# First pieces of x on ScalarE's queue, a one-column warm tile, and 512-column last sums in a two-layer decoder trunk

## The chip, the cores and the metric

One Trainium2 chip; the kernel runs on one of its cores. The metric is the device time of one execution in microseconds, given as the median of several runs. TensorE (PE) does the matmuls and loads its weights in a stream of its own (PEld), VectorE is DVE, ScalarE is ACT, GpSimd is POOL, and SyncE (SP) issues DMAs. "L137" is line 137 of the kernel before.

## What is computed

The reference runs two layers over x of 256 tokens by 1024 columns. Each layer is a token mixer and a SwiGLU block, each followed by a residual and a layer norm:

```python
for l in range(DEPTH):          # DEPTH = 2
    mix = hybrid_mixer(x, w_in[l], w_branch_sb[l], w_branch_moba[l], w_out[l])
    x = layer_norm(DEEPNORM_ALPHA * x + mix, ln_mix_g[l], ln_mix_b[l])
    ffn = swiglu(x, w_ffn_gate[l], w_ffn_up[l], w_ffn_down[l])
    x = layer_norm(DEEPNORM_ALPHA * x + ffn, ln_ffn_g[l], ln_ffn_b[l])

def swiglu(x, w_gate, w_up, w_down):
    return (jax.nn.silu(x @ w_gate) * (x @ w_up)) @ w_down   # inner width 2816
```

The mixer projects x to the queries, keys and values of two kinds of attention and to two gates. Everything is float32.

## The kernel before

**Three matmuls for one product.** A float32 operand is cut into a high part, in a rounded float32 format (float32r), and the low rest. ACT casts the high part (`act`, L50-53), DVE subtracts it (`dve`, L55-58). A product is then three matmuls, high by high, high by low and low by high (`mm3`, L334). The page puts all of ACT's and DVE's work under L51 and L56, and nearly all matmuls under L328, so tiles are told apart by name.

**The weights** come in 244 granules of 128 x 1024 (512 KB). `WeightStream.load` (L132) issues each granule's DMA on SP's queue, the first four granules of all in two halves of 256 KB (`_pieces`, L127). Up to six raw granules are held (NRAW). `line` (L144) casts and subtracts each granule into a ring of ten. A planner (`Weave`) keeps an estimated time of each engine and thereby writes the order of the instructions by hand; on the chip each engine and each queue runs its own list in that order.

**The start.** x comes transposed in pieces, one tile `xT_raw` for each half of the tokens (t = 0, 1). `kcs` (L298) cuts a half in 256, 256 and 512 columns: pieces 0 and 1 are 128 KB, piece 2 is 256 KB. All six are issued on SP's queue, piece (0, 0) before everything, the others between the halves of the granules as `X_AFTER` says (L188, used in `between`, L302). Call the halves of granule 0 w0a and w0b, and so on. SP's order is: x(0,0), w0a, w0b, x(1,0), x(0,1), w1a, w1b, x(1,1), x(0,2), w2a, w2b, x(1,2), w3a, w3b, and on from there with whole granules.

Meanwhile TensorE multiplies zeros: `idle` is a 128 x 512 tile that DVE clears after two small memsets (L279-284), and `N_WARM` = 6 matmuls of it go to a scratch bank (L286-287). ACT runs a sigmoid on one column as its first work (L281).

The first projection (`l0pv`) uses granules 0 to 3. The first two (NWHOLE) are not cut in parts: `whole` (L358) multiplies raw by raw in float32, one such product being two matmul records in the trace. Its eight products, 16 records, run in the order x(0,0) by w0a, by w0b; x(1,0) by w0a, by w0b; then x(0,1) and x(1,1) by w1a and w1b. From granule 2 on `mm3` is used.

**The end.** The last product, by `w_down`, runs over 22 chunks of the inner width (NFC). Of the first 14 (22 less HOLD = 8) each is done for both token halves in turn (L837-840); the last 8 are done for half 0 first, then for half 1, so that the norm of half 0 (`last_norm`, L619) runs on DVE meanwhile. Half 0 sums into two banks of 512 columns (tile `l1pd`). In the last layer half 1 sums into three tiles (`l1pe`): 512 columns, 256 and 256 (L834-835). In `last_norm` for half 1 the remaining 8 chunks go to the 512 columns first, then to one 256, then to the other, and behind each part DVE adds the residual and takes the statistics (`bn_stats`) of those columns. Then follow the aggregate, two small operations on POOL, six operations on DVE and the three stores of that half.

Of the kernel before, what the change touches and what calls it, by code (L numbers as in the profile page):

```python
# [7 lines left out]
F32 = mybir.dt.float32  # L8
F32R = mybir.dt.float32r
AF = mybir.ActivationFunctionType  # L10
# [4 lines left out]
P = 128  # L15
# [8 lines left out]
NFC = D_FF // P  # L24
# [13 lines left out]
class Weave:  # L38
# [16 lines left out]
    def dve(self, e, n, f, *args, **kw):  # L55
        f(*args, **kw)  # L56
        self.dve_t = max(self.dve_t, e) + n / 960.0 + DVE_FIXED
        return self.dve_t + HOP

    def pool(self, e, f, *args, **kw):  # L60
        f(*args, **kw)
        self.pool_t = max(self.pool_t, e) + 0.3
        return self.pool_t + HOP
# [121 lines left out]
RING = 10 * GCOLS + LINES  # L185
NRAW = 6
NWHOLE = 2
X_AFTER = {(0, 1): ((1, 0), (0, 1)), (1, 1): ((1, 1), (0, 2)), (2, 1): ((1, 2),)}  # L188
NSPLIT = 10
HOLD = 8  # L190
N_WARM = 6
LEAD = 2
BACKLOG = 0.37
HOP = 0.21
# [19 lines left out]
def hybrid_trunk_kernel(ctx: ExitStack, tc: tile.TileContext, w, xT_in, x_in, ln_in,  # L214
                        ident_in, mask_in, rope_in, out):
    nc = tc.nc

    big = ctx.enter_context(tc.tile_pool(name="big", bufs=1))
# [10 lines left out]
    def unit(name, shape, dt=F32):  # L229
        return acts.tile(shape, dt, tag="u4", name=name)  # L230
# [10 lines left out]
    def bankM(name, shape):  # L241
        return psM.tile(shape, F32, tag="M", name=name)

    def bankC(name, shape):
        return psC.tile(shape, F32, tag="C", name=name)
# [13 lines left out]
    zero, mhalf = few[:, 0:1], few[:, 1:2]  # L259
# [8 lines left out]
    act, dve, pool = weave.act, weave.dve, weave.pool  # L268


    xT_raw = [unit(f"xT_raw{t}", [P, KC, P]) for t in range(2)]
# [2 lines left out]
    mask = const.tile([P, 2, P], F32, name="mask")  # L274
    warm = small.tile([P, 1], F32, tag="nmu", name="warm")

    nc.gpsimd.memset(ends, 0.0)
    nc.gpsimd.memset(ends[:, P - 1::2 * P], 1.0)
    nc.vector.memset(zero, 0.0)  # L279
    nc.vector.memset(mhalf, -0.5)  # L280
    nc.scalar.activation(warm, zero, AF.Sigmoid)  # L281

    idle = unit("idle", [P, 512], F32R)
    nc.vector.memset(idle.bitcast(F32), 0.0)
    busy = bankC("busy", [P, 512])
    for i in range(N_WARM):  # L286
        nc.tensor.matmul(busy, idle[:, :P], idle, start=True, stop=True)

    def load_xT(t, ks):
        nc.sync.dma_start(xT_raw[t][:, ks, :], xT_in[:, t, ks, :])  # L290

    def split_xT(t, ks):
        n = (ks.stop - ks.start) * P
# [3 lines left out]

    kcs = [slice(0, 2), slice(2, 4), slice(4, 8)]  # L298
    ws.side = weave.add(ws.line(), last=True)
    load_xT(0, kcs[0])  # L300

    def between(g, i):  # L302
        for t, k in X_AFTER.get((g, i), ()):
            load_xT(t, kcs[k])

    ws.load(4, between)
    for k in range(2):
        for t in range(2):
# [25 lines left out]
    def mm3(o, s_hi, s_lo, m_hi, m_lo, start, stop):  # L334
        mm(o, s_hi, m_hi, start, False)
        mm(o, s_hi, m_lo, False, False)
        mm(o, s_lo, m_hi, False, stop)
        weave.tick()
# [8 lines left out]
    def pe_done():  # L347
        return weave.t + HOP
# [50 lines left out]
    def token_out(o, g, t, s_hi, s_lo, first, last):  # L399

        hi, lo = ws.take(g)
        ts = slice(t * P, (t + 1) * P)
        for c0, ps in o:
            cs = slice(c0, c0 + ps.shape[-1])
            mm3(ps, s_hi[:, ts], s_lo[:, ts], hi[:, cs], lo[:, cs], first, last)
# [168 lines left out]
    halves = [slice(h * 512, (h + 1) * 512) for h in range(2)]  # L574

    def residual(e, x, cs, ps, sum_out=None):
        return dve(e, cs.stop - cs.start, nc.vector.scalar_tensor_tensor, x[:, cs], x[:, cs], ALPHA, ps,
                   op0=OP.mult, op1=OP.add, accum_out=sum_out)

    def scale_shift(e, x, cols, sub, op, scale, g, b, e_scale):  # L580

        for c in cols:
            dve(e, c.stop - c.start, nc.vector.scalar_tensor_tensor, x[:, c], x[:, c], sub, g[:, c],
                op0=op, op1=OP.mult)
        for c in cols:
            e = dve(e_scale, c.stop - c.start, nc.vector.scalar_tensor_tensor, x[:, c], x[:, c], scale,
                    b[:, c], op0=OP.mult, op1=OP.add)
            yield c, e

    def norm_line(name, t, junk, gb):  # L590

        x = xs[t]
        st = small.tile([P, 2], F32, tag="st", name=f"{name}_st{t}")
        nmu = small.tile([P, 1], F32, tag="nmu", name=f"{name}_nmu{t}")
        ve = small.tile([P, 1], F32, tag="ve", name=f"{name}_ve{t}")
        e = pe_done()
        for h in range(2):
            e = residual(e, x, halves[h], junk[:, h, :], st[:, h:h + 1])
        e = dve(e, 16, nc.vector.tensor_scalar, nmu, st[:, 0:1], st[:, 1:2], -1.0 / D, op0=OP.add, op1=OP.mult)
        e2 = act(e, D + 100, nc.scalar.activation, junk, x.rearrange("p (h c) -> p h c", h=2), AF.Square,  # L600
                 bias=nmu, accum_out=ve)
        e2 = pool(e2, nc.gpsimd.tensor_scalar, ve, ve, 1.0 / D, EPS, op0=OP.mult, op1=OP.add)
        e2 = pool(e2, nc.gpsimd.tensor_tensor, ve, ve, mhalf, op=OP.pow)
        ends = [e for _, e in scale_shift(e, x, halves, nmu, OP.add, ve, *gb, e2)]
        for h in range(2):
            yield ends[h] + MARGIN
            tp = bankC(f"{name}_tp{t}{h}", [P, 4, P])
            pe_after(ends[h])
            for j in range(4):
                transpose(tp[:, j, :], x[:, (4 * h + j) * P:(4 * h + j + 1) * P])  # L610
            ks = slice(h * 4, (h + 1) * 4)
            ts = slice(t * P, (t + 1) * P)
            e = pe_done()
            yield e
            xT_ready[t] = yield from split_line(xT_hi[:, ks, ts], xT_lo[:, ks, ts], tp, 512, e)
# [3 lines left out]
    def last_norm(name, t, banks, gb, down):  # L619

        x = xs[t]
        st = small.tile([P, 3, 6], F32, tag="bn", name=f"{name}_bn{t}", bufs=1)
        mv = small.tile([P, 2], F32, tag="mv", name=f"{name}_mv{t}", bufs=1)
        ve = small.tile([P, 1], F32, tag="ve", name=f"{name}_ve{t}")
        cols = [slice(c0, c0 + ps.shape[-1]) for c0, ps in banks]
        if t == 0:
            down(banks)
        for i, (c0, ps) in enumerate(banks):
            if t == 1:
                down([(c0, ps)])  # L630
            residual(pe_done(), x, cols[i], ps)
            e = dve(0.0, cols[i].stop - c0, nc.vector.bn_stats, st[:, i, :], x[:, cols[i]])
        e = dve(e, 16, nc.vector.bn_aggr, mv, st[:, :len(banks), :])
        e2 = pool(e, nc.gpsimd.tensor_scalar, ve, mv[:, 1:2], EPS, None, op0=OP.add)
        e2 = pool(e2, nc.gpsimd.tensor_tensor, ve, ve, mhalf, op=OP.pow)
        for c, _ in scale_shift(e, x, cols, mv[:, 0:1], OP.subtract, ve, *gb, e2):
            nc.sync.dma_start(out[t * P:(t + 1) * P, c], x[:, c])
# [17 lines left out]
    for l in range(DEPTH):  # L655
        G = l * NG_LAYER
        L = f"l{l}"
# [19 lines left out]
        else:  # L677
            for t in range(2):
                weave.finish(norms[:t + 1])
                pe_after(xT_ready[t])  # L680
                for j, put in enumerate((put_v, put_q)):
                    ps = bankM(f"{L}pvq{j}{t}", [P, WIDTH])
                    for i in range(4):
                        g = G + 4 * j + i
# [68 lines left out]
        for c in range(KC):  # L753
            g = G + 40 + c
# [3 lines left out]
            ps = bankM(f"{L}pb{c}", [P, 2, S])  # L758
# [7 lines left out]
            e = dve(0.0, S, nc.vector.tensor_add, mt[:, 0, :], mt[:, 0, :], mt[:, 1, :])  # L766
# [15 lines left out]
        def h_parts(c):  # L782
            return h_t[c // 4][0][:, c % 4, :], h_t[c // 4][1][:, c % 4, :]
# [27 lines left out]
        for t in range(2):  # L811
            weave.finish(norms[:t + 1])
            pe_after(xT_ready[t])
            for j in range(2):
                ps = bankM(f"{L}pft{t}{j}", [P, 512])
                for i in range(4):
                    g = G + 56 + 4 * j + i
# [4 lines left out]
        for c in range(NTOK_FC, NFC):  # L822
            ps = bankM(f"{L}pf{c}", [P, 2, S])
# [7 lines left out]
        acc = [banksB(f"{L}pd{t}") for t in range(2 if l < DEPTH - 1 else 1)]  # L831
        banks = [[(512 * h, a[:, h, :]) for h in range(2)] for a in acc]
        if l == DEPTH - 1:
            banks.append([(0, bankM(f"{L}pe0", [P, 512])), (512, bankM(f"{L}pe1", [P, 512])[:, :256]),  # L834
                          (768, bankC(f"{L}pe2", [P, 512])[:, :256])])
        g = G + 100
        for c in range(NFC - HOLD):  # L837
            for t in range(2):
# [1 line left out]
            ws.used(g + c)  # L840
        norms = []
        for t in range(2):
            def down(part, t=t):
                for c in range(NFC - HOLD, NFC):
                    token_out(part, g + c, t, *h_parts(c), False, c == NFC - 1)
                    if t == 1:
                        ws.used(g + c)
            if l < DEPTH - 1:
                down(banks[t])
                norms.append(weave.start(norm_line(f"{L}b", t, acc[t], gb)))  # L850
            else:
                last_norm(f"{L}b", t, banks[t], gb, down)
# [86 lines left out]
```

## Time and profile before

| what | value |
|---|---|
| median of 3 runs | 734.23 us (734.13 to 734.25) |
| profiled execution: its time / its span | 734.21 us / 732.4 us |
| mean granted TensorE clock in it | 0.998 |
| PE busy | 723.1 us (99%) |
| DVE busy / ACT busy | 515.6 us (70%) / 384.5 us (52%) |
| moved by DMA | 136.32 MB, mean 186 GB/s |

The span is what the trace covers; 1.81 us of the execution's time lie around it. PE stands at 9 tenths or more in all 40 slices of the page, so the time of this kernel is the sum of TensorE's work and of the few places where TensorE waits. The timeline lists, for each run of like instructions, the start, the time covered, engine, line, operation, and in brackets the idle time before it with what ended it. The chain of waits follows the work that ended last back in time. The times of single matmuls include a drain that overlaps the next one, so that costs of matmuls are read from the distance between starts.

### The profile page before, as it was taken

To read this page: it belongs to the slowest core of one execution; us is meant where nothing else is said; L and a number is where in the kernel's file an instruction comes from. 1 tells how busy PE (TensorE), PEld (TensorE's weight loads), DVE (VectorE), ACT (ScalarE), POOL (GpSimd) and SP (SyncE) were. 2 spreads that over 40 slices of the span, in tenths; PEclk is the share of its full clock that TensorE was granted. 3 is DMA by queue.
4 is the path that set the end of the run, shared out by engine and by line. 5 is a ranking of instruction groups with operands and counts; after the bars stand their busy time and mean duration, and the time that the engine had idled before them with its cause. 6 is when DMAs were issued, how large, how long until landed. Compare 5 with 4: busy or idle time off the path is not lost.

```text
span 732.4 us, 12739 instructions
## 1 busy us (share of the span) xinstructions
PE 723.1 (99%) x5136; PEld 664.7 (91%) x5136; DVE 515.6 (70%) x723; ACT 384.5 (52%) x570; POOL 14.8 (2%) x30
## 2 busy tenths in 40 slices
PE   9999999999999999999999999999999999999996
PEld 5898999998799999988889989999888999998885
DVE  4988877795886666644578897777578766656416
ACT  5755668743565455533356566675246645445300
POOL 0000000000000000000000000000010000000001
PEclk9999999999999999999999999999999999999999
DMA  8953553863586655476158425457436866554601
GB/s 319 353 202 116 163 191 122 263 241 117 176 279 211 198 201 186 160 273 215 57 177 286 144 96 190 147 158 257 161 115 223 264 203 193 186 172 129 244 1 57
DMA packets 39226, 136.32 MB, mean 186 GB/s; under 512 B 4480, under 2 KB 5504, under 8 KB 39168
## 3 DMA queue, kind: packets, MB, share of 16 engines
q1 hardware_dynamic: 39168, 135.51, 54.9%
q8 instruction: 40, 0.66, 0.3%
q14 instruction: 18, 0.15, 0.1%
HBM read 134.45 MB, written 1.05 MB: 185 GB/s over the span
## 4 chain that ended last, share of the span: by engine, by line
PE 95%; DVE 2%; issue 1%; ACT 1%; POOL 1%; POOLq 0%; DVEq 0%
PE l1pf L328 13%; PE l0pf L328 13%; PE l0pd L328 8%; PE l1pg L328 6%; PE l0pg L328 6%; PE l1pe L328 4%; PE l1pd L328 4%; PE l0pq L328 3%; PE l0pk L328 3%; PE l1pk L328 3%; PE l1pvq L328 3%; PE l1pb L328 3%; PE l0pb L328 3%; PE l1pw L328 2%; PE l0pw L328 2%; PE l0pft L328 2%
## 5 line engine op out<-in xcount | busy, mean ns | idle before, releaser
L56 DVE TENSOR_TENSOR wlo<-raw,whi 128x1024 fp32r<-128x1024 f32 (+1 forms) x244 | 292.1, 1214 | 77.1 <-ACT whi L51 74.2
L51 ACT CAST whi<-raw 128x1024 fp32r<-128x1024 f32 (+1 forms) x244 | 249.8, 1042 | 68.4 <-PE l0pd L328 19.1
L328 PE MATMUL l0pf<-xT_hi,whi 128*128 128x256 f32 x288 | 79.6, 276 | 0.0
L328 PE MATMUL l1pf<-xT_hi,whi 128*128 128x256 f32 x288 | 79.6, 276 | 0.0
L328 PE MATMUL l0pf<-xT_lo,whi 128*128 128x256 f32 x288 | 79.5, 276 | 0.0
L328 PE MATMUL l0pf<-xT_hi,wlo 128*128 128x256 f32 x288 | 79.5, 276 | 0.0
L328 PE MATMUL l1pf<-xT_lo,whi 128*128 128x256 f32 x288 | 79.5, 276 | 0.0
L328 PE MATMUL l1pf<-xT_hi,wlo 128*128 128x256 f32 x288 | 79.5, 276 | 0.0
L328 PEld LDWEIGHTS l0pf<-xT_lo,whi 128*128 128x128 f32 x288 | 54.1, 188 | 0.0
L328 PEld LDWEIGHTS l1pf<-xT_lo,whi 128*128 128x128 f32 x288 | 54.1, 188 | 0.0
L328 PEld LDWEIGHTS l1pf<-xT_hi,whi 128*128 128x128 f32 x288 | 54.1, 188 | 0.0
L328 PEld LDWEIGHTS l0pf<-xT_hi,whi 128*128 128x128 f32 x288 | 54.1, 188 | 0.0
L328 PEld LDWEIGHTS l0pf<-xT_hi,wlo 128*128 128x128 f32 x288 | 54.1, 188 | 0.0
L328 PEld LDWEIGHTS l1pf<-xT_hi,wlo 128*128 128x128 f32 x288 | 54.1, 188 | 0.0
L328 PE MATMUL l1pg<-xT_hi,whi 128*128 128x256 f32 x128 | 36.0, 281 | 0.0
L328 PE MATMUL l0pg<-xT_hi,whi 128*128 128x256 f32 x128 | 36.0, 281 | 0.0
L328 PE MATMUL l1pg<-xT_lo,whi 128*128 128x256 f32 x128 | 35.5, 277 | 0.0
L328 PE MATMUL l1pg<-xT_hi,wlo 128*128 128x256 f32 x128 | 35.5, 277 | 0.0
L328 PE MATMUL l0pg<-xT_lo,whi 128*128 128x256 f32 x128 | 35.5, 277 | 0.0
L328 PE MATMUL l0pg<-xT_hi,wlo 128*128 128x256 f32 x128 | 35.4, 277 | 0.0
L328 PE MATMUL l0pd<-whi,l0h_hi 128*128 128x512 f32 x88 | 34.4, 391 | 0.0
L328 PE MATMUL l0pd<-whi,l0h_lo 128*128 128x512 f32 x88 | 34.3, 389 | 0.0
(403 smaller groups left out, 1763.9 us busy)
## 6 DMA issues: line engine op xcount, KB each, us to landing
raw<-in_w_dram SPq DMA_DIRECT2D x240, 512.0 KB, 4.2
ln<-in_ln_dram SPq DMA_DIRECT2D x8, 512.0 KB, 6.2
raw<-in_w_dram SPq DMA_DIRECT2D x8, 256.0 KB, 4.9
x<-in_x_dram SPq DMA_DIRECT2D x2, 512.0 KB, 5.3
out_dram<-x SPq DMA_DIRECT2D x3, 256.0 KB, 2.0
xT_raw<-in_xT_dram SPq DMA_DIRECT2D x4, 128.0 KB, 4.4
xT_raw<-in_xT_dram SPq DMA_DIRECT2D x2, 256.0 KB, 4.8
out_dram<-x SPq DMA_DIRECT2D x2, 128.0 KB, 1.9
```

Of the source, the lines that this page charges most:

```text
L51: f(*args, **kw)
L56: f(*args, **kw)
L328: nc.tensor.matmul(o, a, b, start=start, stop=stop)
```

## The change

- **First loads.** x(0,0), x(1,0) and x(0,1) are issued on ACT's queue, ahead of ACT's sigmoid. SP's queue begins with w0a; its order becomes w0a, w0b, w1a, w1b, x(1,1), w2a, x(0,2), w2b, x(1,2), w3a, w3b.
- **Warming.** `idle` is a tile of 128 x 1, cleared as DVE's first instruction, and read as a broadcast for both operands. There are 5 warming matmuls in place of 6, still 512 columns wide. The tile lies in another pool.
- **Last sums.** Half 1 sums into two banks of 512 columns for chunks 0 to 13, as half 0 does. Of the last 8 chunks it does all into the first 512 columns, then chunks 14 to 17 into the second bank at 512 columns, then chunks 18 to 21 (FINE = 4) into columns 512-767 of that bank, and last the same four chunks for columns 768-1023 into a fresh 256-column tile `rest`. DVE adds the residual to columns 768-1023 from the second bank while `rest` is summed, then adds `rest` with one more operation.

```diff
-X_AFTER = {(0, 1): ((1, 0), (0, 1)), (1, 1): ((1, 1), (0, 2)), (2, 1): ((1, 2),)}
+X_AFTER = {(1, 1): (1, 1), (2, 0): (0, 2), (2, 1): (1, 2)}
...
+FINE = 4
-N_WARM = 6
+N_WARM = 5
...
+    idle = big.tile([P, 1], F32R, name="idle")
+    nc.vector.memset(idle.bitcast(F32), 0.0)
+    busy = bankC("busy", [P, 512])
+    for i in range(N_WARM):
+        nc.tensor.matmul(busy, idle.to_broadcast([P, P]), idle.to_broadcast([P, 512]), start=True, stop=True)
...
-    nc.scalar.activation(warm, zero, AF.Sigmoid)
-    idle = unit("idle", [P, 512], F32R)
-    nc.vector.memset(idle.bitcast(F32), 0.0)
-    busy = bankC("busy", [P, 512])
-    for i in range(N_WARM):
-        nc.tensor.matmul(busy, idle[:, :P], idle, start=True, stop=True)
...
-    load_xT(0, kcs[0])
+    for t, k in ((0, 0), (1, 0), (0, 1)):
+        load_xT(t, kcs[k], nc.scalar)
+    nc.scalar.activation(warm, zero, AF.Sigmoid)
...
+            cols = [halves[0], slice(512, 768), slice(768, 1024)]
+            (_, first), (_, second) = banks
+            rest = bankC(f"{name}_rest", [P, 512])[:, :256]
+            down([(0, first)])
+            residual(pe_done(), x, cols[0], first)
+            dve(0.0, 512, nc.vector.bn_stats, st[:, 0, :], x[:, cols[0]])
+            down([(512, second)], NFC - HOLD, NFC - FINE, last=False)
+            down([(512, second[:, :256])], NFC - FINE)
+            residual(pe_done(), x, cols[1], second[:, :256])
+            dve(0.0, 256, nc.vector.bn_stats, st[:, 1, :], x[:, cols[1]])
+            residual(pe_done(), x, cols[2], second[:, 256:])
+            down([(768, rest)], NFC - FINE, first=True)
+            dve(pe_done(), 256, nc.vector.tensor_add, x[:, cols[2]], x[:, cols[2]], rest)
+            e = dve(0.0, 256, nc.vector.bn_stats, st[:, 2, :], x[:, cols[2]])
...
-            banks.append([(0, bankM(f"{L}pe0", [P, 512])), (512, bankM(f"{L}pe1", [P, 512])[:, :256]),
-                          (768, bankC(f"{L}pe2", [P, 512])[:, :256])])
+            banks.append([(512 * h, bankM(f"{L}pe{h}", [P, 512])) for h in range(2)])
```

More of the change, by code (lines that the diff above doesn't have):

```diff
@@ L280, in hybrid_trunk_kernel, with load_xT @@
     nc.vector.memset(mhalf, -0.5)
-    nc.scalar.activation(warm, zero, AF.Sigmoid)
-    idle = unit("idle", [P, 512], F32R)
-    nc.vector.memset(idle.bitcast(F32), 0.0)
-    busy = bankC("busy", [P, 512])
-    for i in range(N_WARM):
-        nc.tensor.matmul(busy, idle[:, :P], idle, start=True, stop=True)
-    def load_xT(t, ks):
-        nc.sync.dma_start(xT_raw[t][:, ks, :], xT_in[:, t, ks, :])
+    def load_xT(t, ks, queue):
+        queue.dma_start(xT_raw[t][:, ks, :], xT_in[:, t, ks, :])
     def split_xT(t, ks):
@@ L299, in hybrid_trunk_kernel @@
     ws.side = weave.add(ws.line(), last=True)
-    load_xT(0, kcs[0])
+    for t, k in ((0, 0), (1, 0), (0, 1)):
+        load_xT(t, kcs[k], nc.scalar)
+    nc.scalar.activation(warm, zero, AF.Sigmoid)
     def between(g, i):
-        for t, k in X_AFTER.get((g, i), ()):
-            load_xT(t, kcs[k])
+        if (g, i) in X_AFTER:
+            t, k = X_AFTER[g, i]
+            load_xT(t, kcs[k], nc.sync)
     ws.load(4, between)
@@ L624, in last_norm @@
         ve = small.tile([P, 1], F32, tag="ve", name=f"{name}_ve{t}")
-        cols = [slice(c0, c0 + ps.shape[-1]) for c0, ps in banks]
         if t == 0:
+            cols = halves
             down(banks)
[L628 to L633, printed above, removed]
+            for i, (c0, ps) in enumerate(banks):
+                residual(pe_done(), x, cols[i], ps)
+                e = dve(0.0, 512, nc.vector.bn_stats, st[:, i, :], x[:, cols[i]])
+        else:
+            cols = [halves[0], slice(512, 768), slice(768, 1024)]
[12 more added lines that the diff above has]
+            e = dve(0.0, 256, nc.vector.bn_stats, st[:, 2, :], x[:, cols[2]])
+        e = dve(e, 16, nc.vector.bn_aggr, mv, st[:, :len(cols), :])
         e2 = pool(e, nc.gpsimd.tensor_scalar, ve, mv[:, 1:2], EPS, None, op0=OP.add)
@@ L842, in hybrid_trunk_kernel, with down @@
         for t in range(2):
-            def down(part, t=t):
-                for c in range(NFC - HOLD, NFC):
-                    token_out(part, g + c, t, *h_parts(c), False, c == NFC - 1)
+            def down(part, c0=NFC - HOLD, c1=NFC, first=False, last=True, t=t):
+                for c in range(c0, c1):
+                    token_out(part, g + c, t, *h_parts(c), first and c == c0, last and c == NFC - 1)
                     if t == 1:
```

## The prediction

> **What bounds the kernel now.** I read the page first, then the chain of waits for both ends, TensorE's waits in between, and the timeline of the first 16 and the last 14 us.
>
> ```profile
> span 732.4 us, 12739 instructions
> PE 723.1 (99%) x5136; PEld 664.7 (91%) x5136; DVE 515.6 (70%) x723; ACT 384.5 (52%) x570; POOL 14.8 (2%) x30
> ```
>
> TensorE is busy for 723.1 of 732.4 us. Between 14 and 700 us the table of waits has two lines for PE, of 0.3 us each:
>
> ```profile
> PE l0a_tp L341 <- DVE xT_lo L56: 0.3, 1, 0.3
> PE l1a_tp L341 <- DVE xT_lo L56: 0.3, 1, 0.3
> ```
>
> So whatever starts the stream of matmuls sooner, or makes it shorter, should move the end by as much. The change does the one in the first 12 us and the other in the last 70. The start, in the chain of waits and in the timeline (SPq rows are DMA issues, in the order of the code; "x2" covers two):
>
> ```profile
> 4.42 7.61 PE l0pv L362 x16
> 12.04 5.45 PE l0pv L328 x24
> ```
>
> ```profile
> 0.72 1.28 ACT L281 ACT_TABLE_LOAD   x1 [0.72 <-PEq L925]
> 0.72 0.38 SPq L290 DMA_DIRECT2D xT_raw<-in_xT_dram  x1
> 0.79 0.06 DVE L279 MEMSET few<- 128x1 f32 x1 [0.79 <-PEq L925]
> 1.16 0.89 SPq L137 DMA_DIRECT2D raw<-in_w_dram  x2
> 1.50 2.93 PE L287 MATMUL busy<-idle 128*128 128x512 f32 x6 [1.50 <-DVE idle L284]
> 2.10 0.91 SPq L290 DMA_DIRECT2D xT_raw<-in_xT_dram  x2
> 3.80 0.63 PE L287 MATMUL busy<-idle 128*128 128x512 f32 x1
> 4.22 1.11 PE L362 MATMUL l0pv<-raw,xT_raw 128*128 128x512 f32 x1
> 5.13 0.66 PE L362 MATMUL l0pv<-raw,xT_raw 128*128 128x512 f32 x1
> 5.44 0.38 PEld L362 LDWEIGHTS l0pv<-raw,xT_raw 128*128 128x128 f32 x2 [0.82 <-DMA raw<-in_w_dram]
> 6.59 0.33 SPq L290 DMA_DIRECT2D xT_raw<-in_xT_dram  x1
> 6.62 0.30 PEld L362 LDWEIGHTS l0pv<-raw,xT_raw 128*128 128x128 f32 x2 [0.80 <-DMA xT_raw<-in_xT_dram]
> 7.15 0.19 PEld L362 LDWEIGHTS l0pv<-raw,xT_raw 128*128 128x128 f32 x1 [0.24 <-issue]
> 11.02 0.19 PEld L362 LDWEIGHTS l0pv<-raw,xT_raw 128*128 128x128 f32 x1 [0.24 <-issue]
> ```
>
> Warming holds TensorE until 4.22. Record 1 of 16 then runs at half pace: record 2 starts 0.91 later, while from 7.15 to 11.02 nine records go by at 0.43 each. Record 3 waits for w0b (weights at 5.44, so the matmul at about 5.63), record 5 for x(1,0) (6.62, matmul at about 6.72). From there nothing is missing: 12 x 0.43 more, and the 16 are through at 11.88 (the chain's 4.42 + 7.61 has a drain of 0.15 on top). The limit in this stage is the landing of w0b and of x(1,0). From issue to landing, in the views by tile, x(0,0), w0a, w0a with w0b, and x(1,0) took:
>
> ```profile
> DMA to landing us min/median/max: 2.6/2.6/2.6
> DMA to landing us min/median/max: 2.9/2.9/2.9
> DMA to landing us min/median/max: 2.9/3.3/3.8
> DMA to landing us min/median/max: 4.5/4.5/4.5
> ```
>
> So x(0,0) is there at 3.3, w0a at 4.06, w0b (issued at 1.6) at 5.4, x(1,0) at 6.6.
>
> **Part 1: the warming.** `idle` becomes DVE's first instruction, at 0.79 for 0.06; matmuls should start at about 0.90, against 1.50. Six start within 3.80 - 1.50 = 2.30, 0.43 apart but for the first, whose weight load nothing covers. Five then end their turn at 0.90 + 2.30 = 3.20, in place of 4.22. A broadcast operand stands in no row; I take it at the price of the plain tile. Bounds: not below 0.43 a matmul, since the columns streamed are the same, and at twice that, 5.4 would be the end of warming, record 3 would come at about 6.3, record 5 at 7.1, and the start would lose 0.4. The former is nearer, as shape and type are those of the row. The memsets that now come behind it have no reader before ACT's sigmoid. At best this part removes a cover that is no longer needed: by itself it gains nothing unless the data land sooner.
>
> **Part 2: the first loads.** On SP's queue w0a moves from 1.16 to 0.72 and w0b from 1.6 to 1.16; on ACT's, x(1,0) moves from 2.10 to about 1.16. ACT pays three issues of some 0.45 us ahead of its table load (1.28 us): that ends near 3.3 in place of 2.0, then the sigmoid of 0.2 us, so that the first cast of x, which today starts when x(0,0) lands, comes 0.2 us late. Its reader is the `mm3` part near 12 us; free, with 8 us of cover.
>
> How much of the earlier issue arrives? The busy share and rate of the DMA engines by stretch (second last and last column):
>
> ```profile
> 4.25:5.25 1.00, 1.00 (x3) 0.36 (x2) 0.00 (x0) 0.00 (x0) 0.00 (x0) 1.00 0.56 173
> 7.25:8.25 1.00, 1.00 (x4) 0.47 (x3) 0.55 (x2) 0.09 (x1) 0.00 (x0) 1.00 0.95 346
> ```
>
> Just before x(1,0) lands the engines stand half idle, at 173 GB/s against 346 later, so there is room that a second queue can fill. But the pieces now travel side by side: 128 KB at 346 GB/s are 0.38 us that w0a and w0b may lose to x. I take half of that. w0a lands at 0.72 + 2.9 + 0.2 = 3.85 (ends 3.62 and 4.1), so record 1 starts at 3.85 and record 2 at 4.76. w0b lands at 1.16 + 3.8 + 0.2 = 5.2 (4.98 to 5.4), so record 3 starts at 5.4, record 4 at 5.83, record 5 at 6.26, provided x(1,0) is in: 1.16 + 4.5 = 5.66, with 0.6 to spare. The 16 end at 6.26 + 5.16 = 11.42 in place of 11.88: 0.46 gained. The ends: w0b at 4.98 gives 0.68; w0b no sooner than now gives 0.23; w0b late by 0.38 gives -0.15. I take 0.40, a little under the middle, because a landing counts when the slowest engine is done.
>
> The Trainium skill, page "DMA: Bandwidth & Descriptors", section "Issuing engines are not separate DMA queues", speaks against this part: DMAs of several issuing engines interleave on the same 16 engines, and a second issuer only saves the sequencer's issue time, usually small beside the transfer. By that sentence alone the first 655 kB would land when they do now and the 0.40 would be about 0; the half-idle second above is why I don't go by it.
>
> What is late next is the cut of granule 2, with which `mm3` begins:
>
> ```profile
> 9.38 0.41 ACT L51 CAST xT_hi<-xT_raw 128x256 fp32r<-128x256 f32 x1 [0.22 <-DMA xT_raw<-in_xT_dram]
> 10.00 1.29 ACT L51 CAST whi<-raw 128x512 fp32r<-128x512 f32 x2 [0.22 <-DMA raw<-in_w_dram]
> 10.65 1.36 DVE L56 TENSOR_TENSOR wlo<-raw,whi 128x512 fp32r<-128x512 f32 x2 [0.41 <-ACT whi L51]
> ```
>
> The first half of the low part is there at 11.33, the second at 12.0, which the fifth matmul of `mm3` needs, 0.9 after the first: no wait as long as `mm3` starts at 11.1 or later. 11.42 fits even if granule 2 lands no sooner.
>
> **Part 3: the last sums.** These are matmul counts by pitch. The sums of the first layer are 512 wide throughout, and their row in the chain gives 55.11 / 243 = 0.2268 us a matmul. The 14 interleaved chunks of the last layer, and the two last stretches:
>
> ```profile
> 304.65 55.11 PE l0pd L328 x243
> 664.21:703.13 38.92, 38.92 (x211) 33.67 (x211) 17.11 (x16) 14.34 (x15) 0.00 (x0) 1.00 0.41 150
> 703.13 10.91 PE l1pd L328 x48
> 714.03 11.20 PE l1pe L328 x72
> ```
>
> (211 is 14 x 15 and one at the edge.) After, 14 x 12 matmuls at 0.2268 are 38.10: **0.82** gained. Half 0's 48 come to 10.89: 0.01. Half 1's 72 become 36 wide and 24 narrow ones. The narrow pitch, and DVE's part behind the last matmul:
>
> ```profile
> 719.31 0.28 PE L328 MATMUL l1pe<-whi,l1h_hi 128*128 128x256 f32 x1
> 724.95 0.28 PE L328 MATMUL l1pe<-whi,l1h_lo 128*128 128x256 f32 x1
> 725.26 0.42 DVE L56 SCALAR_TENSOR_TENSOR x<-x,l1pe 128x256 f32<-128x256 f32 x1 [1.99 <-PE l1pe L328]
> 725.72 0.43 DVE L56 BATCH_NORM_STATS2 l1b_bn<-x 128x6 f32<-128x256 f32 x1
> 726.18 0.24 DVE L56 BATCH_NORM_AGGREGATE l1b_mv<-l1b_bn 128x2 f32<-128x18 f32 x1
> ```
>
> 47 pitches in 5.64 us are 0.120. So 24 narrow ones become 12 wide ones: 24 x 0.120 - 12 x 0.2268 = **0.16** gained. Weights cover it: the splitting of granules is ahead of TensorE here, with ACT busy 14.34 of 38.92.
>
> DVE gets one more operation. Behind the last matmul stand an addition and the statistics, as now; the addition's price I take from the 0.42 of the residual, which also reads 256 columns of a bank. The extra residual must be done before `rest` is. DVE starts 0.31 after the start of the last matmul of columns 512-767 and needs three operations 0.46 apart: ready at 1.69. `rest` is ready for it 12 x 0.120 + 0.31 = 1.75 after that same start. The cover is 0.06; if it is gone, the loss is the overshoot, 0.1 at most.
>
> **Sum.** 0.82 + 0.01 + 0.16 + 0.40 = 1.39 off the span: 731.0. The profiled execution took 734.21, 1.81 more than its span, and stands 0.02 under the median of 734.23, so **732.8**. I take 0.2%, 1.47 us, as what a measurement of this kernel tells from no change; the forecast falls just short of it.
>
> **Rivals.** *A: the data land no sooner.* Two queues share the engines, and the start gains nothing: 734.23 - 0.99 = 733.2. (The sentence of the Trainium skill under part 2 comes to this.) One more row speaks for it: SP's twelfth load, at 6.59, started when the fourth, x(1,0), landed (2.10 + 4.5).
>
> ```profile
> SPq L290 <- DMA xT_raw<-in_xT_dram: 0.7, 1, 0.7
> ```
>
> If eight loads may be under way over both queues, x(0,2), then the tenth, waits for the second, x(1,0), until 5.7 or later; it is issued at 4.5 now. Taking 4.9 as now (9.4 - 4.5), it lands at 10.6, and cast and cut (0.41, 0.65, 0.68) are done at 12.3, where the second `mm3` matmul runs at 12.10 now: a loss of 0.2, thus 733.4. Against it: with fewer loads ahead x(0,2) should be faster than 4.9, as the first load's 2.6 beside the fourth's 4.5 shows.
>
> *B: the clock stays down; slower.* Today matmuls run without a gap from 1.50, and the full pace comes at about 5.1, some 3.6 us later. After the change warming ends at 3.20 and TensorE idles until 3.85. If that gap spoils the stretch on which the clock is judged, and the next ends 3.6 later at 8.7, then (8.7 - 3.85) / 0.91 = 5.3 records are done by then, and the other 10.7 take 4.6: through at 13.3, 1.4 later than now, against 0.99 gained at the end: 734.6. It outweighs the end once the clock comes later than about 7.9 us. Against it: the gap is a fifth of the stretch, and today's stretch, too, would have begun before 1.50 unless it lies just so. The Trainium skill, page "TensorE: Matmul & The Clock Gate", section "What's actually happening", has a free-running window of 3413 ns that must be busy; by that figure the next chance is near 8.5 and the time, as an estimate, 734.5. No row says how full a window must be.
>
> *C: the start gains more.* If w0b comes at once with w0a and the clock by 4.6, the records run from 3.85 with about 0.4 lost: end near 11.1, gain 0.8: 732.4. The cut of granule 2 then decides.
>
> *D: the wide matmuls keep the slow pitch.* In the last layer's stretch the 512-wide ones take more than 0.2268: if that came from something other than their narrow neighbours, 0.3 to 0.4 of the 0.82 stay: 733.2.
>
> **How the numbers follow.** Forecast (start gains 0.2 to 0.7) 0.56; A 0.18; B 0.10; C 0.10; D 0.06. The range is 732.2 to 734.0: it holds forecast, C, A and D, and leaves out B and the outer edges. Faster by over 0.2% are C and the nearly half of the forecast in which the start gives 0.48 or more: 0.36. Slower by over 0.2% needs more than B's price: 0.02. The rest, 0.62, is within.
>
> **What would show it.** Right: warming from 0.90 to about 3.2; record 1 near 3.85, record 5 near 6.3; `l0pv` under L328 from about 11.4; `l1pd` and `l1pe` in sixes of 1.36; the last stretch some 11.0; DVE's addition 0.31 behind the last matmul. Wrong: records 0.9 apart beyond 5.4 (B); the weights of record 5 still waiting at 6.6 or of `mm3` past 11.5 (A); 1.39 a six (D).

## The result and the profile after

The kernel after takes 741.85 us (median of 5 runs, 741.66 to 742.16). The kernel before, run on the same chip between them, takes 734.25 (734.13 to 734.85). The ratio is 1.0101, with a 95% interval of 1.0087 to 1.0115: slower by 7.6 us, where I had forecast 1.4 faster. The profiled execution took 742.16 with a span of 740.4, 8.0 more than before's 732.4. The head of the page:

```profile
span 740.4 us, 12630 instructions
PE 730.9 (99%) x5081; PEld 665.4 (90%) x5081; DVE 516.0 (70%) x724; ACT 384.3 (52%) x570; POOL 14.8 (2%) x30
```

TensorE does 55 matmuls fewer and is busy 7.8 us longer. It still waits for nearly nothing, so matmuls that existed before have become slower. (The page of the kernel before has PE at 9 tenths in 39 of the 40 slices and at 6 in the last, behind the last matmul, not at 9 in all 40.) The chain of waits of the kernel after, its start and some of its long pieces (start, us, what):

```profile
0.72 3.61 DMA xT_raw<-in_xT_dram
4.33 0.04 issue
4.37 9.57 PE l0pv L364 x16
13.94 5.46 PE l0pv L330 x24
...
140.29 22.71 PE l0pb L330 x192
163.00 17.49 PE l0pw L330 x75
212.55 95.91 PE l0pf L330 x846
308.46 56.70 PE l0pd L330 x243
```

and the same long pieces in the chain of the kernel before:

```profile
137.94 21.76 PE l0pb L328 x192
159.70 17.03 PE l0pw L328 x75
208.75 95.90 PE l0pf L328 x846
```

The change does not touch the middle of the kernel, and yet `l0pb` takes 0.95 more, `l0pw` 0.46 more, and `l0pd` 56.70 in place of the 55.11 shown above: 0.2333 a matmul, not 0.2268. `l0pf` is as it was. The end, in the same chain:

```profile
671.53 1.41 PE l1pd L330 x6
672.94 1.40 PE l1pe L330 x6
...
710.74 11.20 PE l1pd L330 x48
721.94 9.82 PE l1pe L330 x48
731.76 1.43 PE l1b_rest L330 x12
```

Four differences make up the 8.0. The first `mm3` matmul starts at 13.37 in the timeline, where it was 11.47 before: 1.90. From there to the last layer's sums, which begin at 671.53 in place of 664.21, another 5.42 are lost. The sums last 731.76 + 1.43 - 671.53 = 61.66, before 714.03 + 11.20 - 664.21 = 61.02: 0.64. Behind the last matmul 0.05 is added. The start in detail, from the timeline of the kernel after:

```profile
0.72 1.37 ACTq L289 DMA_DIRECT2D xT_raw<-in_xT_dram  x3
0.79 0.06 DVE L279 MEMSET idle<- 128x1 f32 x1 [0.79 <-PEq L939]
0.91 2.50 PE L282 MATMUL busy<-idle 128*128 128x512 f32 x5 [0.91 <-DVE few L286]
...
4.37 9.57 PE L364 MATMUL l0pv<-raw,xT_raw 128*128 128x512 f32 x16 [0.97 <-DMA xT_raw<-in_xT_dram]
...
8.80 0.34 PEld L364 LDWEIGHTS l0pv<-raw,xT_raw 128*128 128x128 f32 x1 [0.52 <-issue]
...
9.48 0.19 PEld L364 LDWEIGHTS l0pv<-raw,xT_raw 128*128 128x128 f32 x1 [0.35 <-issue]
```

The warming is as the prediction has it: `idle` cleared at 0.79, the matmuls from 0.91, 2.50 long with the drain of the last. But x(0,0) lands at 4.33, not 3.3 as before, and TensorE waits 0.97 for it. A weight load of 0.34 is one at half pace, one of 0.19 at full pace: the half-pace ones go on to 8.80, with records 0.85 apart, and full pace is there at 9.48. Before, the first full-pace load stood at 7.15. The trace also records when the granted clock changes: it comes to full at 9.30, in the kernel before at 5.26. (That record begins with this change, so the means of the granted clock, 0.997 and 0.998, leave the half pace at the start out.)

### The profile page after: what moved, and what is told of

Its sections match the earlier page's. It is cut to its first block, busy times and chain, and to the rows that moved or that the text cites. A ratio compares the mean times of both kernels' runs of the same rounds, so it can differ in the third digit from the quotient of the medians.

```text
span 740.4 us, 12630 instructions
## 1 busy us (share of the span) xinstructions
PE 730.9 (99%) x5081; PEld 665.4 (90%) x5081; DVE 516.0 (70%) x724; ACT 384.3 (52%) x570; POOL 14.8 (2%) x30
## 4 chain that ended last, share of the span: by engine, by line
PE 95%; DVE 2%; issue 1%; ACT 1%; POOL 1%; DMA 0%; POOLq 0%; DVEq 0%
PE l0pf L330 13%; PE l1pf L330 13%; PE l0pd L330 8%; PE l0pg L330 6%; PE l1pg L330 6%; PE l1pd L330 4%; PE l1pe L330 4%; PE l1pb L330 3%; PE l0pb L330 3%; PE l0pk L330 3%; PE l1pk L330 3%; PE l0pq L330 3%; PE l1pvq L330 3%; PE l0pw L330 2%; PE l1pw L330 2%; PE l0pft L330 2%
```

## The experiments

Two theories of where the time went. **Places:** the new four-byte tile `idle` lies in the pool `big`, ahead of the raw granules, the activations, the constants and the work tiles. In the built program it takes 32 bytes, so that all of those begin 32 bytes further: the raw granules, the activations and all but the small ones of the others 32 bytes past a multiple of 256 in place of at one. The ring and `xT` do not move. That slows matmuls by some per cent. **Clock:** the gap between warming and the first record keeps TensorE at half pace longer (rival B). Rivals to the first: the broadcast operands, the new sums, or the loads on ACT's queue slow something in the middle. Where no other kernel is named, an experiment is an edit of the kernel before.

### The tile and the warming

**The kernel after, without the new tile** (a_few): the column lies in a tile that was there already.

```diff
-    idle = big.tile([P, 1], F32R, name="idle")
+    idle = few[:, 2:3].bitcast(F32R)
```

> The changed kernel, but the warming column is a spare column of the tile few, so that no tile is added in front of the others. Address theory: the added tile pushes everything behind it (raw granules, and the pool that holds the inner activations) 32 bytes along, and matmuls with an operand there run some 3% slower; those stages cost 7.0 us in all (5.4 between 14 and 664 us, 1.6 in the last sums). Then this kernel takes 741.85 - 7.0 = 734.8, with the sums of the first layer back at 0.2268 us a matmul and the late clock at the start left in. Rival, slot order: the old 512-column tile took one place in the ring of activation slots, and without it the tiles meet in other slots; that is unchanged here, so 741.8 and 0.234 us a matmul stay.

Measured: 735.17, ratio 1.0008 (0.9999 to 1.0018) to before's 734.47. This one line is worth 6.7 of the 7.6. In its chain:

```profile
210.67 95.90 PE l0pf L330 x846
306.57 55.11 PE l0pd L330 x243
...
715.12 9.59 PE l1pe L330 x48
724.71 1.45 PE l1b_rest L330 x12
```

`l0pd` is back at 55.11. This kernel keeps the broadcast operands, the new sums and the loads, so none of these three slows the middle, and the slot order of the expectation does not either. The last sums begin where `l1pf` ends (570.23 + 95.90 = 666.13) and end at 726.16, 60.03 in all and 1.00 less than before. The start still loses: the first `mm3` matmul starts at 13.37 again.

**The kernel before, with 32 bytes, and with 64 bytes, added to `big`** (b_pad32, b_pad64), and nothing else:

```diff
     wlo = big.tile([P, RING], F32R, name="wlo")
+    pad = big.tile([P, 8], F32, name="pad")      # 16 in b_pad64
+    nc.vector.memset(pad, 0.0)
```

> The kernel before with one unused tile of 32 bytes a partition behind the weight rings, nothing else. Address theory: 734.2 + 5.4 + about 1.5 = 741, with the sums of the first layer at 0.234 us a matmul and the start as before. Slot order, or anything that the new loads or sums bring: 734.2.

> As the one with 32 bytes, but 64. If an operand must start on a 64-byte boundary: 734.2. If what counts is its place within 256 bytes, or against the other operand: 741 or something between, with some stages slow and others not.

Measured: 741.0 with 32 bytes, ratio 1.0086 (1.0070 to 1.0103), and 748.98 with 64 (one run). A tile that nobody reads costs 6.5 and 14.5 us. With 32 bytes `l0pd` takes 56.71 in the chain, as in the kernel after. With 64 bytes `l0pf` suffers too, and `l0pg` takes some 0.7 longer by the distances between starts:

```profile
211.51 99.64 PE l0pf L330 x846
311.16 56.69 PE l0pd L330 x243
```

**The kernel after without the new tile, with eight warming matmuls** (a_few_w8):

```diff
-N_WARM = 5
+N_WARM = 8
```

> As the first of these four, with 8 warming matmuls in place of 5, so that TensorE has no gap before the first record: warming ends at 4.5. Clock theory (the gap from 3.2 to 4.4 spoiled the stretch on which the clock is judged): full pace by about 5, record 5 at about 6.4, the 16 records through at about 11.6 in place of 13.8, and 734.8 - 2.2 = 732.6. Rival (the clock comes late because of where the warming starts, or because of the broadcast operand): records stay 0.85 apart until 9 and the time is 734.8 or a little more.

Measured: 733.26, ratio 0.9984 (0.9974 to 0.9993), 1.9 less than with five. The timeline has no wait ahead of the first record, and half pace ends sooner:

```profile
0.91 3.78 PE L282 MATMUL busy<-few 128*128 128x512 f32 x8 [0.91 <-DVE few L286]
...
4.61 8.27 PE L364 MATMUL l0pv<-raw,xT_raw 128*128 128x512 f32 x16
...
6.47 0.34 PEld L364 LDWEIGHTS l0pv<-raw,xT_raw 128*128 128x128 f32 x1 [0.52 <-issue]
7.13 0.19 PEld L364 LDWEIGHTS l0pv<-raw,xT_raw 128*128 128x128 f32 x1 [0.32 <-issue]
```

### Each part alone

**The last sums alone** (b_sums): the change's edits in `last_norm`, `banks` and `down`.

> The kernel before with the last sums of the change alone; no tile moves in on-chip memory. The sum of the prediction for this part: 0.99 less, so a ratio of 0.9987 to the kernel before on the same chip, with l1pd and l1pe in sixes of 1.36 and the 256-column tile at 1.43 + 1.43. Rival (the slow pitch of the wide matmuls in that stretch has another cause than the narrow neighbours): 0.6 less at most, sixes of 1.39.

Measured: 733.55 against 734.41, ratio 0.9992 (0.9982 to 1.0001). By itself that does not stand apart from no change; the trace does show the gain: the sums begin at 665.05 and end at 725.08, 60.03 long, as without the new tile above.

**The warming alone** (b_warm5): five matmuls from one column of `few`, loads on SP.

```diff
+    idle = few[:, 2:3].bitcast(F32R)             # first memset of DVE, 5 broadcast matmuls
...
-    idle = unit("idle", [P, 512], F32R)          # and 6 matmuls
```

> The kernel before with the warming of the change alone (one column, from a spare column of few; 5 matmuls), loads on SP as before. If the clock is judged over a stretch of about 3.4 us that must be filled, at places that do not depend on the kernel, the gap from 3.2 to 4.1 puts full pace between 7.5 and 10.9 instead of between 4.9 and 8.3: some 1.3 us more, ratio 1.0015 to 1.002. If the gap does not matter: 0 to 0.2 less, as only the landing of w0b and x(1,0) binds.

Measured: 735.53, ratio 1.0015 (1.0006 to 1.0024). The wait for w0a opens a gap, and full pace comes late, though all data arrive as before:

```profile
4.06 9.10 PE L361 MATMUL l0pv<-raw,xT_raw 128*128 128x512 f32 x16 [0.65 <-DMA raw<-in_w_dram]
...
7.61 0.34 PEld L361 LDWEIGHTS l0pv<-raw,xT_raw 128*128 128x128 f32 x1 [0.52 <-issue]
8.28 0.19 PEld L361 LDWEIGHTS l0pv<-raw,xT_raw 128*128 128x128 f32 x1 [0.34 <-issue]
```

**The loads alone** (b_loads): three pieces of x on ACT's queue, with the old tile and six matmuls.

```diff
-    load_xT(0, kcs[0])
+    for t, k in ((0, 0), (1, 0), (0, 1)):
+        nc.scalar.dma_start(xT_raw[t][:, kcs[k], :], xT_in[:, t, kcs[k], :])
+    nc.scalar.activation(warm, zero, AF.Sigmoid)
```

> The kernel before with the loads of the change alone, warming as before (1.5 to 4.2). From the trace of the changed kernel: x(0,0) and w0a land at about 4.4 (not 4.1), w0b and x(1,0) at about 5.4 (not 6.6). If the gap of 0.2 does not spoil the clock: between 0.3 less and 0.1 more, ratio 0.9996 to 1.0002. If even that spoils it: full pace only from 7.8 on, 1.2 more, ratio 1.0016.

Measured: 734.34, ratio 1.0000 (0.9991 to 1.0009). The loads gain nothing and, with warming until 4.2, lose nothing.

**The sums, with seven matmuls from one column, loads on SP** (b_warm7_sums):

> A version that may beat both: last sums of the change, one-column warming from 0.9 with 7 matmuls, which end at 4.07 when w0a lands, all loads on SP. 0.99 less for the sums and, as warming starts 0.6 earlier and the clock comes that much earlier on average, 0.3 less for the start: ratio 0.9982.

Measured: 733.15, ratio 0.9985 (0.9976 to 0.9994): with a_few_w8 the fastest of all kernels here, 0.15% under the kernel before. What the seven warming matmuls add to the sums alone (733.55) does not stand apart from nothing. Warming now lasts until the data are there. The chain is that of the fastest of its ten executions, at 732.63, and has the 16 records through early:

```profile
0.92 3.34 PE busy L282 x7
4.26 7.11 PE l0pv L362 x16
11.37 5.49 PE l0pv L328 x24
```

**The same, with x(0,0) on SP and x(1,0) and x(0,1) on ACT's queue** (b_mix), to see whether the loads gain once the clock is kept:

> The best kernel so far (last sums 512 wide; seven warming matmuls from one column of a tile that was there; 733.15, ratio 0.9985) with two of the first pieces of x, (1,0) and (0,1), on ScalarE's queue and the first one left on SP's. If the second queue helps when TensorE has no gap and the first piece keeps its 2.6 from issue to landing: w0b and x(1,0) come sooner, about 0.3 less, 732.8, ratio 0.998. If the landings are shared and nothing is gained: 733.15, ratio 0.9985. If a third theory, that the clock alone sets the start, holds, the time goes with the moment of full pace: 0.3 either way.

Measured: 735.48, ratio 1.0009 (1.0000 to 1.0018), some 1.8 more than without this edit by the two ratios. Neither of the first two theories had that. From its timeline:

```profile
3.52 0.71 ACT L51 CAST xT_hi<-xT_raw 128x256 fp32r<-128x256 f32 x2 [0.38 <-DMA xT_raw<-in_xT_dram]
4.99 9.01 PE L364 MATMUL l0pv<-raw,xT_raw 128*128 128x512 f32 x16 [0.72 <-DMA raw<-in_w_dram]
6.52 0.65 PEld L364 LDWEIGHTS l0pv<-raw,xT_raw 128*128 128x128 f32 x2 [1.06 <-DMA raw<-in_w_dram]
...
8.53 0.34 PEld L364 LDWEIGHTS l0pv<-raw,xT_raw 128*128 128x128 f32 x1 [0.52 <-issue]
```

The cast of x(0,0) and of x(1,0) stands at 3.52, so both are there by 3.9, and x(1,0) came at 6.6 before. But w0a takes 3.68 from issue to landing (1.17 to 4.85 in the chain) where it took 2.9, and w0b is there only at 6.5. What x wins, the weights lose. The 1.06 is idle time of the weight stream alone: records 2 and 3 start at 5.97 and 6.83, 0.86 apart as at half pace elsewhere, so the matmuls have one gap, of 0.72. Half pace lasts beyond 8.53, so the third theory (the start goes with the moment of full pace) has the sign, with far more than its 0.3. How much of the 1.8 is the clock and how much the late record 1 (4.99 in place of 4.26), no run separates.

### Which tiles count

A whole 256 bytes, the activations with all behind them, the raw granules alone, the constants and work tiles alone, the activations alone:

```diff
+    pad = big.tile([P, 64], F32, name="pad")                    # b_pad256
...
+    gap = wpool.tile([P, 8], F32, tag="gap", name="gap")        # b_acts32: behind the raw granules
...
+    pad = big.tile([P, 8], F32, name="pad")                     # b_raw32: 32 ahead of them,
+    gap = wpool.tile([P, 56], F32, tag="gap", name="gap")       #   224 behind
...
+    edge = const.tile([P, 8], F32, name="edge")                 # b_back32
...
+    gap = wpool.tile([P, 8], F32, tag="gap", name="gap")        # b_only32: 32 ahead of the
+    edge = const.tile([P, 56], F32, name="edge")                #   activations, 224 behind
```

(Each is zeroed once and not read.) b_raw64 and b_acts64 are b_raw32 and b_acts32 with 64 bytes, for `l0pf`.

> The kernel before with a tile of 256 bytes added at the end of the pool `big` and zeroed once, so that every tile behind it moves by a whole 256 bytes. Address theory (what counts is where a matmul operand begins within 256 bytes): as before, 734.4, ratio 1.000 within 0.002, and the 243 matmuls of l0pd take 55.1 in the chain. Rival (any tile between the ring and the activations costs, by moving the activations to other rows of the memory): 740 to 749, with l0pd at 56.7.

> The kernel before with a tile of 32 bytes added behind the raw granules, so that the raw granules stay where they were and the activations and all behind them move by 32 bytes. Theory (the activations are operands of TensorE and their place sets the pitch): all of the loss that the 32-byte tile in `big` showed, 741.0, ratio 1.0086, l0pd 56.7. Rival (the raw granules, which ScalarE and VectorE read and the DMA writes, are what slows TensorE): 734.4, ratio 1.000, l0pd 55.1.

> The kernel before with a tile of 32 bytes ahead of the raw granules and one of 224 bytes behind them, so that only the raw granules begin 32 bytes past a multiple of 256 and all behind them moves by a whole 256. Theory (the place of the activations counts): 734.4, ratio 1.000 within 0.002, l0pd 55.1. Rival (the raw granules count): 741.0, l0pd 56.7. A split would show as a part of the 6.6 here and the rest in the kernel that moves the activations alone.

> As the one before with 64 bytes ahead of the raw granules and 192 behind. With 64 bytes ahead of both, l0pf took 101.84 instead of 98.11 in start-to-start distances although neither of its operands had moved. If the raw granules' place did that (they are read by ScalarE and VectorE and written by the DMA while l0pf runs): l0pf 101.8 and l1pf 101.8 here, and a time about 7 longer than before, 741.5. If the activations' place did it (the products of l0pf are evicted into them): l0pf 98.1 and 734.4.

> The kernel before with a tile of 32 bytes ahead of the constants, so that only what lies behind the activations (constants, work tiles, small tiles) begins 32 bytes further. If the operands' place is the cause, the stages of l0pd, l0pw and l0pb keep their pace (55.1, 17.0 and 21.8 in the chain), since their operands lie in the activations and the ring: about 734.4. If the tiles behind (written by ScalarE and VectorE while TensorE runs) are the cause: up to 741.0. A stage whose operands never moved, l0pk with 11.10 instead of 10.88, may go with either.

> The kernel before with 32 bytes ahead of the activations and 224 behind them, so that the activations alone begin 32 bytes past a multiple of 256. If their place is the cause: the whole loss, 741.0, l0pd 56.7, l0pb 22.7, l0pw 17.5. If it needs the tiles behind too: less, down to 734.4.

> The kernel before with 64 bytes ahead of the activations, the raw granules where they were. With 64 bytes ahead of both, l0pf rose from 95.9 to 99.6 in the chain and the time to 749.0, though neither operand of l0pf moved; the raw granules alone at 64 bytes left l0pf at 95.9. If the activations and what lies behind them do it: 749, l0pf 99.6. If it takes both: l0pf 95.9 and about 741.5, from l0pd, l0pw and l0pb alone.

| kernel | us | ratio, or the kernel before beside it | l0pb | l0pw | l0pf | l0pd |
|---|---|---|---|---|---|---|
| b_pad256 | 734.26 | 0.9998 (0.9988 to 1.0008) | 21.76 | 17.03 | 95.90 | 55.11 |
| b_raw32 | 734.57 | 1.0000 (0.9990 to 1.0009) | 21.76 | 17.03 | 95.90 | 55.11 |
| b_raw64 | 735.07, one run | 734.53 | 21.76 | 17.03 | 95.90 | 55.11 |
| b_acts32 | 741.04 | 1.0089 (1.0074 to 1.0104) | 22.71 | 17.49 | 95.91 | 56.70 |
| b_only32 | 739.34, one run | 734.75 | 22.71 | 17.49 | 95.90 | 56.70 |
| b_back32 | 735.64, one run | 734.75 | 21.76 | 17.03 | 95.91 | 55.11 |
| b_acts64 | 749.54, one run | 734.75 | 23.04 | 17.50 | 99.64 | 56.69 |

(The last four columns are pieces of each kernel's chain.) The chain of b_only32, in which the activations alone have moved, beside that of b_back32:

```profile
137.74 22.71 PE l0pb L332 x192
160.45 17.49 PE l0pw L332 x75
209.98 95.90 PE l0pf L332 x846
305.88 56.70 PE l0pd L332 x243
...
719.11 11.29 PE l1pe L332 x72
```

```profile
48.53 6.35 PE l0pk L330 x51
...
139.01 21.76 PE l0pb L330 x192
160.77 17.03 PE l0pw L330 x75
209.85 95.91 PE l0pf L330 x846
305.76 55.11 PE l0pd L330 x243
```

A whole 256 bytes costs nothing, so it is the place within 256 bytes that counts (0, 32 and 64 were tried, 128 was not). The raw granules cost nothing at 32 or 64. At 32 the activations carry the large part: `l0pb`, `l0pw` and `l0pd` lose exactly what they lose in the kernel after. What lies behind them costs some 0.2 in `l0pk` (6.35 in place of 6.14) and the like in three other stages, 0.8 together by the distances between starts in the trace. By the same distances the activations carry 5.5, and the two parts come to the 6.3 or so of b_acts32. At 64 bytes the two were only moved together (b_acts64).

## Why the prediction was wrong

**The warming, part 1: the step that failed.** I priced `idle` by what it is used for: one memset, five matmuls, "at best this part removes a cover that is no longer needed". I did not price what its allocation moves, and no rival did. The shifted places cost 5.42 up to the last sums, and in these 61.66 - 60.03 = 1.63 more: 7.05 of the span's 8.0, and 6.7 of the median as a_few shows. The profile of before could not show it, since there all these tiles begin at a multiple of 256 bytes; the declaration of the tile in the diff, beside the order of the pools, could have raised the question. So could the weight stream: `shift` (L206) lays some granules of the ring 16 columns, 64 bytes, further than the others, and `_lay` all others at a multiple of 256 bytes, a sign that such places matter. The rest of part 1 held: warming from 0.91, and the broadcast operand at the price of the plain tile (five in 2.50 with the drain).

**The first loads, part 2: wrong in sign.** I had w0a as the last to come for record 1, at 3.85. On ACT's queue, beside the weights, x(0,0) took 3.61 in place of 2.6, and record 1 waited for it until 4.37: 0.52 later. (w0a took 3.4, not 2.9 and 0.2, and was there at 4.1.) The clock did the rest, by rival B's mechanism, to which I gave 0.10 and which I argued away with "the gap is a fifth of the stretch". B had the next full pace at 8.7 and a loss of 1.4. Measured: half pace to 8.80, and `mm3` at 13.37. The profiled execution of before was lucky: in eleven profiled executions with its start (its own, and those of edits that leave the start as it is but for a memset) `mm3` began between 11.18 and 12.57, 11.99 in the mean, and against that the loss is 1.4. By medians it is 1.7 (a_few is 0.70 slower with sums that gain 1.00). B's gap alone, with the loads where they were, gave +0.15% (b_warm5); its absence gave back 1.9 (a_few_w8). The record of the granted clock agrees: full clock comes between 4.75 and 7.68 in the eleven; with a gap it comes at 9.30 (the kernel after), 9.14 (a_few), 8.83 (b_mix) and 8.09 (b_warm5), and with warming up to the data at 6.92 (a_few_w8) and 4.24 (b_warm7_sums). That the gap spoils the clock is thus shown. (The `mm3` starts here are those of a first record that lies over the last of the 16: it is 0.79 long, the next ones 0.40. The 16 themselves are through at about 11.88 before, as the prediction has it, 0.41 behind that start; in the kernel after, by the same 0.41, at about 13.78, where B had 13.3.)

The Trainium skill, page "DMA: Bandwidth & Descriptors", section "Issuing engines are not separate DMA queues", which I set aside for the half-idle second before 5.25, was right: b_loads measured 1.0000, and in b_mix the weights lost what x won. The Trainium skill, page "TensorE: Matmul & The Clock Gate", section "What's actually happening", has the window free-running, and the change of pace variable for it by some 500 ns either way; here, with one and the same start, the clock came to full anywhere between 4.75 and 7.68 in those eleven executions, which is nearer to the whole window of 3413 ns that the page gives. The traces bear this figure out: in all 18 of them the stretch at full clock lasts a whole number of 3413 ns, 211 to 216. In b_only32 full clock came 3.22 after the first warming matmul (1.53 to 4.75), less than a window, so a window need not be busy from end to end.

**The last sums, part 3: right.** Forecast 0.82 + 0.01 + 0.16 = 0.99; measured 1.00, once the places are undone. (10.91 - 10.89 is 0.02, not 0.01; nothing hangs on it.) The sixes took 1.36 there; the 1.40 of the kernel after, which my text would have read as a part of rival D, was the place. The extra residual was covered, as worked out (0.06 of cover forecast). In the timeline of the kernel after, DVE is free 0.21 before `rest` is done:

```profile
732.60 0.40 DVE L56 SCALAR_TENSOR_TENSOR x<-x,l1pe 128x256 f32<-128x256 f32 x1
733.22 0.42 DVE L56 TENSOR_TENSOR x<-x,l1b_rest 128x256 f32<-128x256 f32 x1 [0.21 <-PE l1b_rest L330]
```

**Rivals A, C, D.** A (data no sooner) was half of the truth: no gain, and more than that, since x(0,0) came later. Its remark on eight loads under way held: on SP's queue the next load, w2a, was issued at 4.34, when x(0,0) had landed at 4.33. C and D did not happen. The whole: +1.7 at the start, -1.0 at the end, +6.7 from places, 7.4 against the measured 7.6.

## What to carry to other kernels

A new tile is not only what is written to it: look at which tiles it pushes, and where their beginnings then lie within 256 bytes; put a small new value into a tile that is there, or give it 256 bytes, and so leave all others where they lay. Where stages that a change does not touch become slower by a few per cent, compare the built addresses before looking for contention. Warm TensorE until the first data are surely there: one warming matmul too many costs, as an estimate from the distance of the starts, no more than 0.43, while a gap of 0.65 cost 1.1 (b_warm5) and filling one of 1.11 gave back 1.9 (a_few_w8).

## What the runs showed of the hardware

- The distance between matmuls depends on where the activations begin within 256 bytes. A matmul reads a stationary operand, held in TensorE, and a moving one, streamed through it. In `l0pd` (512 columns) the activations are stationary, and the weights in the ring begin at a multiple of 256: 0.2268 with the activations at 0, 0.2333 at 32 or 64. In `l0pb` (256 columns) the activations are moving, and the weights lie 64 bytes past a multiple: 0.1133 at 0, 0.1183 at 32, 0.1200 at 64 (21.76, 22.71 and 23.04 over 192).
- A multiple of 256 is not the best place everywhere. The narrow sums of `l1pe` (256 columns, stationary activations, the weights at 0) take 0.120 in the kernel before, with the activations at 0. At 32 they are quicker: of the 11.29 in b_only32 the 24 wide ones take 5.60 at 0.2333, which leaves 0.1185 for each of the 48. So of these two stages of 256 columns each is slowest, 0.120, with both operands at the same place, `l1pe` at 0 and `l0pb` at 64; `l0pd`, with 512 columns, was fastest with both at the same place. That fits a rule about the two places together rather than about one of them. It is not shown, since no run moves the ring.
- `l0pf` went from 0.1133 to 0.1178 a matmul with the activations, and the tiles behind them, at 64 bytes, although its own operands, `xT` and the ring, lie where they lay. The distances are even in the trace (113, 113, 114 ns in turn before; 117 to 119 then), so it is no occasional collision with what ScalarE or VectorE write. The kernel before has the slow distance too: the 18 `l0pf` matmuls ahead of the 846 take 2.12, 0.1178 each. What carries it is open, as are `l0pg` and `l0pk`, of which `l0pk` goes with the tiles behind the activations. So that the place of the operands is the mechanism in `l0pd`, `l0pw` and `l0pb` fits, and is argued only; that at 32 bytes the place of the activations is the cause there is shown.
- Two queues do not add up at the start: with the first pieces of x on a second queue w0a took 3.68 in place of 2.9 from issue to landing.
